# A hybrid decoder layer on one core: a new order of its opening, its small vectors fetched first on another queue, and the last product block's last columns summed in two banks

## The chip, the cores and the metric
One core of one Trainium2 chip runs one layer in one launch. The metric is the device time in microseconds (us). Of the core's engines, PE (TensorE) multiplies matrices and turns tiles, DVE (VectorE) does elementwise work and sums, ACT (ScalarE) does activations and copies, POOL (GpSimd) does little here, and SP issues nearly all DMAs. Each engine takes its instructions in the order in which they were written. All times below are us from the start of the profile's span, if nothing else is said.

## The reference
`x` is 256 tokens by 1024 features, `c` one vector of 1024. All is float32.

```python
mod = silu(c) @ w_ada + b_ada                       # (1024) @ (1024 x 9216), cut into nine vectors
sh1, sc1, gt1, sh2, sc2, gt2, sh3, sc3, gt3 = split(mod, 9)
y = rmsnorm(h, norm_ffn1) * (1 + sc1) + sh1
h = h + 0.5 * gt1 * swiglu(y, w_ffn1_gu, w_ffn1_down)        # 1024 -> 2816 -> 1024
y = rmsnorm(h, norm_mix) * (1 + sc2) + sh2
q, k, v, gu, gv = split(y @ w_in)                   # 5 x 512
attn = causal_attention(rope(q), rope(k), v)        # 8 heads of 64; one block of 256 covers all tokens
gmlp = gelu(gu) * (tril(w_s) @ layernorm(gelu(gv)) + b_s)    # chunks of 128 tokens
h = h + gt2 * (concat(rmsnorm(attn), rmsnorm(gmlp)) @ w_out)
y = rmsnorm(h, norm_ffn2) * (1 + sc3) + sh3
h = h + 0.5 * gt3 * swiglu(y, w_ffn2_gu, w_ffn2_down)
return rmsnorm(h, norm_final)
```

## The kernel before
The 256 tokens are two tiles `t` of 128. The 1024 features are eight slices `j` of 128. Every weight block of 128 x 1024 is fetched once (512 KB, by SP, into one of eight `raw` tiles) and split into two float32r parts: ACT copies it to `wh`, DVE subtracts to get `wl`. The operand is split likewise (`yh`, `yl`), and a product of 512 columns is three matmuls into one PSUM bank: `wh` with `yh`, `wh` with `yl`, `wl` with `yh` (`mm3`, L383). `wh` and `wl` have ten places each.

**Opening.** The modulation of the first norm (`sh1`, `sc1`) comes slice by slice: for each slice two `w_ada` blocks arrive, DVE multiplies each with `c_row` and sums along the row (`ada_sum`), and two tiny operations make the shift and scale columns (`ada_col`). Meanwhile x is squared and summed (`open_s`), the reciprocal root is taken on POOL (`rstd_of`, L349), x is scaled (`open_x`, tile `xn`), turned by PE into tiles `px` (`open_t`), copied to `xnT`, and modulated by ACT into `yh` and `y` (`open_y`), from which DVE makes `yl` (`open_l`). The first four of the eleven gate/up blocks are multiplied slice by slice (`open_m`): 4 blocks x 2 tiles x 8 slices x 3 = 192 matmuls named `f`, into eight banks. `open_e` and `open_d` fetch, `open_g` makes `wh`, `open_G` makes `wl`, `open_A` begins the activation, and `open_p` turns the identity into a scratch bank, which produces nothing. The order of all these steps is the text `OPEN`: one word per step, and each engine runs what falls to it in that order.

**After the opening** come the other seven gate/up blocks and the down products of the first FFN, then the mixing part, whose order is the text `MIX`, then the second FFN. There, helper `tick()` places the splits and the sums for later gates between the products. In the mixing part `step_gb` makes the gated tile `g` on DVE, `step_gq` takes its mean square on ACT (`mean_sq`) and its root by `rstd_of`, `step_gw` scales it, and `step_mt` has PE turn it (tile `tr_mg`).

**End.** The last three blocks' down products run token tile by token tile and half by half (L1028). After the 18 matmuls of a half, `Chain.residual` (L472) runs on it: DVE multiplies the bank by the gate and adds to `h`, ACT squares and sums, DVE multiplies by the final norm's row. After the second half come the root and the scaling, and the two halves are stored.

`rstd_of` adds eps on DVE where it is given two partial sums, and on POOL where it is given one:

```python
        if len(parts) == 2:
            vec.tensor_scalar(v, parts[0], parts[1], EPS, op0=ALU.add, op1=ALU.add)
        else:
            nc.gpsimd.tensor_scalar(v, parts[0], EPS, None, op0=ALU.add)
        nc.gpsimd.tensor_tensor(r, v, mhalf, op=ALU.pow)
```

In the profile's names L85 is the helper through which all DVE and PE work is written, so tiles are read there by name.

Of the kernel before, what the change touches and what calls it, by code (L numbers as in the profile page):

```python
# [38 lines left out]
d.1.0 p p p p x.0.0.1.a a.0.0 p p t.0.a p p c.0.0 p p p p p p p p p c.1.0 p g.0.0.0.2.v p y.0 p x.1.1.3.v G.0.0.0.1 p
p p k d.1.1 p l.0 G.0.0.1.1 p p g.0.1.0.1.a m.0.0.0.0 a.0.1 a.1.1 c.0.1 c.1.1 e.1.2 g.0.1.1.1.a m.0.0.1.1 G.0.1.0.2  # L40
t.2.a g.1.0.0.2.a e.0.2 y.1 p t.3.v d.2.0 t.1.a l.1 p m.0.1.1.1 p m.0.1.0.1 g.1.1.0.2.a d.2.1 m.0.1.1.0 G.1.0.0.1
m.0.1.0.0 G.1.0.1.1 g.2.0.0.1.a G.1.1.0.1 p m.1.0.0.1 g.2.0.1.1.a m.1.1.0.1 a.1.2 m.1.0.1.0 c.1.2 a.0.2 m.1.0.0.0
G.1.1.1.1 c.0.2 m.0.0.0.1 g.2.1.0.1.a G.2.0.0.1 e.1.3 G.2.0.1.1 m.1.1.1.0 y.2 d.3.0 l.2 g.2.1.1.1.a e.0.3 e.1.4 d.3.1
e.0.4 G.2.1.0.1 G.2.1.1.1 a.1.3 g.3.0.0.1.a g.3.0.1.1.a m.1.1.0.0 m.2.0.1.1 m.1.1.1.1 m.2.1.0.1 a.0.3 c.1.3 c.0.3
d.4.0 m.0.0.1.0 y.3 m.2.0.0.0 m.2.1.1.0 d.4.1 m.2.1.0.0 G.3.0.0.2 m.1.0.1.1 l.3 a.1.4 e.0.5 m.2.0.1.0 m.3.0.1.0
m.3.0.0.0 g.3.1.0.2.a G.3.1.1.1 G.3.1.0.1 e.1.5 m.3.1.1.1 d.5.0 m.2.1.1.1 d.5.1 m.3.1.1.0 c.1.4 a.0.4 g.4.0.0.2.a
c.0.4 e.1.6 y.4 m.3.0.1.1 g.4.1.1.1.a G.4.0.0.2 m.2.0.0.1 g.4.1.0.1.a l.4 m.3.1.0.1 G.4.1.0.2 a.1.5 m.3.1.0.0
m.3.0.0.1 e.0.6 m.4.1.1.1 g.5.0.0.2.a m.4.1.0.1 d.6.0 c.1.5 m.4.0.1.1 m.4.0.1.0 a.0.5 c.0.5 y.5 g.5.1.0.2.a m.4.1.1.0
m.4.0.0.1 d.6.1 m.4.0.0.0 G.5.0.0.2 l.5 m.5.0.0.1 e.1.7 m.5.0.1.0 m.5.0.1.1 G.5.1.1.1 g.6.0.0.2.a G.5.1.0.1 m.5.1.0.1
a.1.6 m.5.0.0.0 a.0.6 m.5.1.1.0 m.4.1.0.0 c.1.6 c.0.6 G.6.0.1.1 e.0.7 m.5.1.1.1 G.6.0.0.1 y.6 l.6 m.5.1.0.0 m.6.0.1.1  # L50
d.7.0 a.1.7 g.6.1.0.2.a G.6.1.0.2 a.0.7 m.6.0.1.0 d.7.1 c.1.7 g.7.0.1.1.a m.6.0.0.0 c.0.7 g.7.0.0.1.v m.6.0.0.1
m.6.1.0.0 G.7.0.0.1 y.7 g.7.1.0.2.a l.7 m.6.1.1.0 G.7.0.1.1 u m.6.1.0.1 m.6.1.1.1 G.7.1.0.1 G.7.1.1.1 m.7.0.0.1
# [1047 lines left out]
```

## Time and profile before

| what | us |
|---|---|
| median of three runs (511.62, 511.62, 513.96) | 511.62 |
| span of the profiled execution, first to last instruction | 509.2 |
| median less span: what lies around the span | 2.4 |
| PE busy in the span | 496.5 (98%) |
| DVE busy | 375.1 (74%) |
| ACT busy | 264.1 (52%) |
| POOL busy | 24.3 (5%) |

The profile gives one execution instruction by instruction. A row of its timeline begins with the start and the duration, then the engine, the line, the operation, what it writes and reads, the sizes, and in brackets how long the engine had been idle before it and who ended that. A row of the chain of waits has a start, a length and what filled it. A row of the view by stretches has, for each engine, busy time and in brackets the number of instructions.

### The profile page before, as it was taken

What the parts mean: (1) busy time and instruction counts of PE and PEld (TensorE: products, weight loads), DVE (VectorE), ACT (ScalarE), POOL (GpSimd) and SP (SyncE); (2) the same over time, 40 slices, a digit from 0 to 9 for tenths busy, and PEclk for the clock granted to TensorE, in tenths of its full rate; (3) what the DMA queues carried; (4) which work ended last, traced back from release to release, by engine and by line L of the source; (5) the groups of instructions that cost most, each with busy time, mean ns of one, the idle gap of its engine ahead of it and who ended that gap; (6) DMA issues with size and microseconds to landing.
All of it is one profiled execution on the core that took longest, in us unless ns stands there. A gap on an engine that the chain in (4) does not pass through costs nothing.

```text
span 509.2 us, 6450 instructions
## 1 busy us (share of the span) xinstructions
PE 496.5 (98%) x2297; PEld 404.7 (79%) x2297; DVE 375.1 (74%) x512; ACT 264.1 (52%) x405; POOL 24.3 (5%) x38
## 2 busy tenths in 40 slices
...
GB/s 281 398 371 376 328 236 340 413 408 325 338 308 314 362 208 207 136 196 322 259 258 242 240 196 287 215 325 331 340 205 189 187 168 202 181 152 1 0 2 82
DMA packets 38018, 126.38 MB, mean 248 GB/s; under 512 B 4449, under 2 KB 4449, under 8 KB 37986
## 3 DMA queue, kind: packets, MB, share of 16 engines
...
## 4 chain that ended last, share of the span: by engine, by line
PE 92%; DVE 2%; issue 2%; DMA 1%; ACT 1%; POOL 1%; SPq 0%; POOLq 0%; ACTq 0%
PE pg L85 39%; PE po L85 21%; PE f L85 8%; PE pw L85 4%; PE pp_gv L85 2%; PE pp_v L85 2%; PE pp_q L85 2%; PE pp_k L85 2%; PE pp_gu L85 2%; PE pa L85 2%; PE psc L85 2%; DMA h<-in_x_dram 1%; PE pv L85 1%; PE pada L85 1%; PE ppT L85 1%
## 5 line engine op out<-in xcount | busy, mean ns | idle before, releaser
L85 PE MATMUL pg<-wh_gu,yh 128*128 128x512 f32 x288 | 115.4, 401 | 0.0
L85 DVE TENSOR_TENSOR wl_gu<-raw_gu,wh_gu 128x1024 fp32r<-128x1024 f32 x72 | 86.8, 1222 | 38.1 <-ACT wh_gu L209 37.9
L85 PE MATMUL pg<-wl_gu,yh 128*128 128x512 f32 x288 | 113.7, 395 | 0.0
L85 PE MATMUL pg<-wh_gu,yl 128*128 128x512 f32 x288 | 113.6, 394 | 0.0
L209 ACT ACTIVATE wh_gu<-raw_gu 128x1024 fp32r<-128x1024 f32 x72 | 74.4, 1055 | 49.3 <-PE po L85 30.6
L85 DVE TENSOR_TENSOR wl_d<-raw_d,wh_d 128x1024 fp32r<-128x1024 f32 x44 | 53.8, 1227 | 28.2 <-ACT wh_d L209 28.1
L85 PE MATMUL po<-wh_d,ah 128*128 128x512 f32 x176 | 69.1, 393 | 0.0
L85 PE MATMUL po<-wh_d,al 128*128 128x512 f32 x176 | 69.0, 392 | 0.0
L85 PE MATMUL po<-wl_d,ah 128*128 128x512 f32 x176 | 69.0, 392 | 0.0
L209 ACT ACTIVATE wh_d<-raw_d 128x1024 fp32r<-128x1024 f32 x44 | 46.4, 1059 | 35.0 <-PE pg L85 25.1
L85 PEld LDWEIGHTS pg<-wl_gu,yh 128*128 128x128 f32 x288 | 54.2, 188 | 12.7
L85 PEld LDWEIGHTS pg<-wh_gu,yl 128*128 128x128 f32 x288 | 54.3, 189 | 11.8
L85 PEld LDWEIGHTS pg<-wh_gu,yh 128*128 128x128 f32 x288 | 54.3, 189 | 11.8
L85 PEld LDWEIGHTS po<-wh_d,ah 128*128 128x128 f32 x176 | 33.1, 188 | 7.2
L85 PEld LDWEIGHTS po<-wl_d,ah 128*128 128x128 f32 x176 | 33.1, 188 | 7.1
L85 PEld LDWEIGHTS po<-wh_d,al 128*128 128x128 f32 x176 | 33.1, 188 | 7.1
L85 DVE SCALAR_TENSOR_TENSOR ada<-ada,c_row 128x1024 f32<-128x1024 f32 x32 | 38.5, 1218 | 0.0
L85 DVE SCALAR_TENSOR_TENSOR acc<-ada,cols,acc 128x1024 f32<-128x1024 f32 x24 | 30.7, 1278 | 0.1
L422 ACT ACTIVATE sg<-pg 128x256 f32<-128x256 f32 x36 | 13.7, 385 | 31.6 <-PE pg L85 31.6
L434 ACT ACTIVATE ah<-pa 128x512 fp32r<-128x512 f32 x22 | 13.2, 598 | 26.1 <-PE pa L85 26.1
L85 PE MATMUL f<-wl_first,yh 128*128 128x512 f32 x64 | 25.4, 396 | 0.9 <-DVE wl_first L85 0.9
L85 PE MATMUL f<-wh_first,yh 128*128 128x512 f32 x64 | 25.6, 400 | 0.0
...
## 6 DMA issues: line engine op xcount, KB each, us to landing
raw_gu<-in_gu_dram SPq DMA_DIRECT2D x72, 512.0 KB, 4.8
raw_d<-in_w_ffn_down_dram SPq DMA_DIRECT2D x44, 512.0 KB, 5.2
ada<-in_w_shsc_dram SPq DMA_DIRECT2D x32, 512.0 KB, 5.0
ada<-in_w_gate_dram SPq DMA_DIRECT2D x24, 512.0 KB, 5.0
raw_ada<-in_w_shsc_dram SPq DMA_DIRECT2D x16, 512.0 KB, 6.8
raw_first<-in_gu_dram SPq DMA_DIRECT2D x16, 512.0 KB, 6.7
raw_wo<-in_w_out_dram SPq DMA_DIRECT2D x8, 512.0 KB, 4.4
raw_inq<-in_w_in_dram SPq DMA_DIRECT2D x4, 512.0 KB, 6.8
```

Source lines behind the costliest of these rows:

```text
L85: return getattr(self.engine, name)(out, *args, **kw)
L209: nc.scalar.activation(wh[:, :n], raw[:, :n], AF.Copy)
L422: nc.scalar.activation(sg, ps[:, 0:256], AF.Silu)
L434: nc.scalar.activation(ah, pv, AF.Copy)
```

## The change
1. `cols` (all small vectors) is fetched first, on ACT's queue and not as third on SP's; the two halves of x follow each other on SP.
2. `OPEN` is written anew. The products go strictly slice by slice, gate/up blocks in pairs. The squares of both token tiles are on DVE and all scaling of x is on ACT. All four turns of x stand together ahead of the first product, with 22 idle turns ahead of them and 5 behind; the idle turns between the products are gone.
3. The turn of x (`open_t`) and the copy out of PSUM (`open_q`) are steps of their own, and slice 0 is modulated straight from the PSUM tile (`open_y`).
4. In slice 0 the matmul with `yl` is the last of the three.
5. The three `1 + scale` operations become one, placed behind the squares; silu of the column form of c goes behind the second slice.
6. `rstd_of` adds eps on DVE in all cases.
7. At the end, in the last half of the last token tile, the last block's products go to two new banks of 256 columns each (12 matmuls of 256 in place of 6 of 512). The residual of the blocks before it is added to `h` on its own, then each 256 columns get their own residual, square and norm row, and three partial sums are added in two steps. The square writes over the residual's scratch tile.
8. Comments are dropped, which moves lines (L85 becomes L84).

```diff
 OPEN = """
-s.1.v p e.1.0 p p p p p p s.0.a p p p p p e.0.0 p p p d.0.0 e.1.1 p x.1.0.1.v e.0.1 p p p d.0.1 x.0.1.3.a a.1.0 p p
...
+e.1.0 e.0.0 d.0.0 d.0.1 s.0.v e.1.1 e.0.1 d.1.0 s.1.v e.1.2 x.0.0.1.a b x.0.1.3.a a.1.0 x.1.0.1.a a.0.0 e.0.2 p p p p
+p p p p p p p p p p p p p p p p p p t.0 x.1.1.3.a c.1.0 c.0.0 t.1 g.0.0.0.1.a d.1.1 t.2 G.0.0.0.1 y.0 t.3 p p p p p
+q.1.v l.0 m.0.0.0.0 g.0.0.1.1.a m.0.0.0.1 q.0.a G.0.0.1.1 q.3.a q.2.v g.0.1.0.1.a m.0.0.1.0 d.2.0 g.0.1.1.1.a
...
-    nc.sync.dma_start(c_one, i["c"])
-    nc.sync.dma_start(h[0], i["x"][0, tsl(0), :])
-    nc.sync.dma_start(cols, i["cols"])
-    nc.sync.dma_start(h[1], i["x"][0, tsl(1), :])
+    nc.scalar.dma_start(cols, i["cols"])
+    nc.sync.dma_start(c_one, i["c"])
+    for t in range(NT):
+        nc.sync.dma_start(h[t], i["x"][0, tsl(t), :])
...
-            nc.gpsimd.tensor_scalar(v, parts[0], EPS, None, op0=ALU.add)
+            vec.tensor_scalar(v, parts[0], EPS, None, op0=ALU.add)
...
-    def mm3(ps, lh, ll, wh, wl, first, last):
+    def mm3(ps, lh, ll, wh, wl, first, last, low_last=False):
+        rest = [(ll, wh), (lh, wl)]
+        if low_last:
+            rest.reverse()
         ten.matmul(ps, lh, wh, start=first, stop=False)
-        ten.matmul(ps, ll, wh, start=False, stop=False)
-        ten.matmul(ps, lh, wl, start=False, stop=last)
+        ten.matmul(ps, *rest[0], start=False, stop=False)
+        ten.matmul(ps, *rest[1], start=False, stop=last)
...
+    def open_q(j, e):
         xnT[j] = op.tile([P, 2, S], F32, tag="xT", name=f"xnT{j}")
+        ks = slice(1 if j == 0 else 0, 2)
         if e == "v":
-            vec.tensor_copy(xnT[j], pv)
+            vec.tensor_copy(xnT[j][:, ks, :], px[j][:, ks, :])
...
-            nc.scalar.activation(d, xnT[j // 2][:, j % 2, :], AF.Identity,
+            nc.scalar.activation(d, (xnT[j // 2] if j else px[0])[:, j % 2, :], AF.Identity,
                                  scale=adacol[1][:, js], bias=adacol[0][:, js])
...
     for t in range(NT):
+        c = Chain(t, "z")
+        z = [unit(f"zo{t}{n}", [P, 512]) for n in range(2)]
+        def add(n, po, o, square=True):
+            s = slice(n * 512 + o.start, n * 512 + o.stop)
+            tmp = unit(f"res_z{t}{s.start}", [P, o.stop - o.start])
+            vec.tensor_tensor(tmp, po, adarow[8][:, s], op=ALU.mult)
+            vec.tensor_tensor(h[t][:, s], h[t][:, s], tmp, op=ALU.add)
+            if square:
+                c.parts.append(mean_sq(h[t][:, s], D, f"z{t}{s.start}", tmp))
+                vec.tensor_tensor(z[n][:, o], h[t][:, s], nrow["nfin"][n][:, o], op=ALU.mult)
         for n in range(2):
-            for b in range(NB - HOLD, NB):
+            apart = (t, n) == (NT - 1, 1)
+            for b in range(NB - HOLD, NB - 1 if apart else NB):
...
+            add(n, f2.po[t][n], slice(0, 512), not apart)
+        if apart:
+            for q in range(2):
+                o = slice(q * 256, q * 256 + 256)
+                pe = psm(f"pe{q}")[:, 0:256]
+                for k in range(2):
+                    ah, al = f2.a[last]
+                    wh, wl = need(("d2", last, k))
+                    mm3(pe, ah[:, k, tsl(t)], al[:, k, tsl(t)], wh[:, 512 + o.start:512 + o.stop],
+                        wl[:, 512 + o.start:512 + o.stop], k == 0, k == 1)
+                add(1, pe, o)
+            v = sm.tile([P, 1], F32, tag="var", name=f"v2_z{t}")
+            vec.tensor_tensor(v, c.parts[0], c.parts[1], op=ALU.add)
+            c.parts = [v, c.parts[2]]
```

**DVE at the start, before** (`h_81` is the second half of x, `xn` its scaled copy, `raw_ada` a block of `w_ada`, `wh_first`/`wl_first` the split of a gate/up block):

```order
L85 SCALAR_TENSOR_TENSOR xn_115,ss_x_116<-h_81 128x1024
L85 TENSOR_SCALAR xn_115<-h_81,r_x_119 128x256
L85 SCALAR_TENSOR_TENSOR raw_ada_0_124,sum_163<-raw_ada_0_124,c_row 128x1024
L85 SCALAR_TENSOR_TENSOR raw_ada_0_144,sum_174<-raw_ada_0_144,c_row 128x1024
L85 TENSOR_TENSOR ada_col_187<-sum_174,cols 128x1
L85 SCALAR_TENSOR_TENSOR ada_col_198<-sum_163,cols 128x1
L85 CAST wh_first_0_201<-raw_first_0_149 128x1024
L85 TENSOR_SCALAR xn_115<-h_81,r_x_119 128x768
L85 TENSOR_TENSOR wl_first_0_202<-raw_first_0_149,wh_first_0_201 128x512
```

and in the changed kernel:

```order
L84 SCALAR_TENSOR_TENSOR xn_119,ss_x_120<-h_80 128x1024
L84 TENSOR_SCALAR v_x_122<-ss_x_120 128x1
L84 SCALAR_TENSOR_TENSOR xn_132,ss_x_133<-h_81 128x1024
L84 TENSOR_SCALAR v_x_135<-ss_x_133 128x1
L84 TENSOR_SCALAR cols<-cols 128x3x8
L84 SCALAR_TENSOR_TENSOR raw_ada_0_111,sum_144<-raw_ada_0_111,c_row 128x1024
L84 SCALAR_TENSOR_TENSOR raw_ada_0_113,sum_147<-raw_ada_0_113,c_row 128x1024
L84 SCALAR_TENSOR_TENSOR ada_col_180<-sum_144,cols 128x1
L84 TENSOR_TENSOR ada_col_182<-sum_147,cols 128x1
L84 TENSOR_TENSOR wl_first_0_190<-raw_first_0_115,wh_first_0_189 128x512
L84 COPY xnT_213<-px_184 128x512
L84 TENSOR_TENSOR yl<-y_0_200,yh 128x256
```

Both squares and the eps now stand on DVE; both scalings of x and the first `wh` copy have left it.

**DVE in the mixing part, before** (`g_2731` and `g_2757` are the gated tiles of the two token tiles, `o_2711` the attention output of the second, `pmx` the gate's products in PSUM):

```order
L85 TENSOR_TENSOR g_2731<-g_2731,ug_2660 128x512
L85 SCALAR_TENSOR_TENSOR o_2711<-o_2711,r_o_2723,row_g_attn_out 128x512
L85 TENSOR_TENSOR g_2757<-pmx_2702,cols 128x256
L85 TENSOR_TENSOR g_2757<-pmx_2726,cols 128x256
L85 TENSOR_TENSOR g_2757<-g_2757,ug_2696 128x512
L85 SCALAR_TENSOR_TENSOR g_2731<-g_2731,r_g_2747,row_g_gmlp_out 128x512
```

and in the changed kernel:

```order
L84 TENSOR_TENSOR g_2697<-g_2697,ug_2626 128x512
L84 TENSOR_SCALAR v_g_2712<-ss_g_2709 128x1
L84 SCALAR_TENSOR_TENSOR o_2677<-o_2677,r_o_2689,row_g_attn_out 128x512
L84 TENSOR_TENSOR g_2723<-pmx_2668,cols 128x256
L84 TENSOR_TENSOR g_2723<-pmx_2692,cols 128x256
L84 TENSOR_TENSOR g_2723<-g_2723,ug_2662 128x512
L84 TENSOR_SCALAR v_g_2730<-ss_g_2727 128x1
L84 SCALAR_TENSOR_TENSOR g_2697<-g_2697,r_g_2713,row_g_gmlp_out 128x512
```

The two `v_g`, which need the square that ACT takes of the `g` just made, have come from POOL into DVE's row.

**DVE at the end, before** (from the last bank of the last token tile on):

```order
L85 TENSOR_TENSOR res_z_4464<-po_3322,ada_row_3447 128x512
L85 TENSOR_TENSOR h_81<-h_81,res_z_4464 128x512
L85 TENSOR_TENSOR zo_4470<-h_81,nfin_3457 128x512
L85 TENSOR_SCALAR v_z_4472<-ss_z_4459,ss_z_4467 128x1
L85 TENSOR_SCALAR zo_4462<-zo_4462,r_z_4473 128x512
```

and in the changed kernel (`pe` are the two new banks):

```order
L84 TENSOR_TENSOR res_z_4422<-po_3288,ada_row_3413 128x512
L84 TENSOR_TENSOR h_81<-h_81,res_z_4422 128x512
L84 TENSOR_TENSOR res_z_4432<-pe_4425,ada_row_3413 128x256
L84 TENSOR_TENSOR h_81<-h_81,res_z_4432 128x256
L84 TENSOR_TENSOR zo_4385<-h_81,nfin_3423 128x256
L84 TENSOR_TENSOR res_z_4445<-pe_4438,ada_row_3413 128x256
L84 TENSOR_TENSOR h_81<-h_81,res_z_4445 128x256
L84 TENSOR_TENSOR zo_4385<-h_81,nfin_3423 128x256
L84 TENSOR_TENSOR v_z_4451<-ss_z_4407,ss_z_4435 128x1
L84 TENSOR_SCALAR v_z_4453<-v_z_4451,ss_z_4448 128x1
```

Five operations behind the bank have become ten, six of them half as wide.

## Rows read from the trace of the kernel before

**Rows 1.** View by stretches: PE, PEld, DVE, ACT, POOL, PEclk, DMA share, GB/s.

```profile
30.00:40.00 10.00, 10.00 (x45) 8.11 (x44) 9.31 (x19) 5.66 (x9) 0.00 (x0) 1.00 1.03 388
200.00:480.00 280.00, 279.71 (x1325) 229.08 (x1325) 201.97 (x259) 156.78 (x253) 13.81 (x18) 1.00 0.63 213
```

**Rows 2.** Chain of waits in order of time, opening.

```profile
16.40 2.29 DVE raw_ada L85 x4
18.86 1.23 DVE wl_first L85
...
22.95 40.44 PE f L85 x174
63.39 4.18 PE pg L85 x18
```

**Rows 3.** Timeline of DVE: the square of the second half of x.

```profile
7.34 1.22 DVE L85 SCALAR_TENSOR_TENSOR xn<-h 128x1024 f32<-128x1024 f32 x1 [1.91 <-DMA h<-in_x_dram]
```

**Rows 4.** Timeline of POOL: the two roots of x.

```profile
8.98 0.57 POOL L357 TENSOR_TENSOR r_x<-v_x,mhalf 128x1 f32<-128x1 f32 x1
10.10 1.40 POOL L357 TENSOR_TENSOR r_x<-v_x,mhalf 128x1 f32<-128x1 f32 x1
```

**Rows 5.** Timeline of ACT: x scaled, modulated, and first split copies.

```profile
11.53 1.33 ACT L592 ACTIVATE xn<-h,r_x 128x768 f32<-128x768 f32 x2 [3.58 <-POOL r_x L357]
...
14.24 0.60 ACT L631 ACTIVATE yh<-xnT,ada_col,ada_col 128x256 fp32r<-128x256 f32 x1
...
15.29 1.16 ACT L654 ACTIVATE wh_first<-raw_first 128x512 fp32r<-128x512 f32 x2
```

**Rows 6.** Timeline of PE: the first product.

```profile
15.51 0.48 PE L85 MATMUL f<-wh_first,yh 128*128 128x512 f32 x1
```

**Rows 7.** Groups of the stretch 13 to 60 by form: count, busy, mean ns, idle before.

```profile
L85 DVE SCALAR_TENSOR_TENSOR raw_ada<-raw_ada,c_row 128x1024 f32<-128x1024 f32 x14 | 16.8, 1218 | 0.0
L85 DVE TENSOR_TENSOR wl_first<-raw_first,wh_first 128x512 fp32r<-128x512 f32 x20 | 13.0, 686 | 0.6 <-ACT wh_first L654 0.5
...
L85 DVE TENSOR_TENSOR yl<-y,yh 128x256 fp32r<-128x256 f32 x8 | 3.4, 424 | 0.2 <-ACT y L631 0.2
```

**Rows 8.** DMA issues of 3.4 to 3.6: count, KB, us from issue to landing.

```profile
raw_first<-in_gu_dram SPq DMA_DIRECT2D x1, 512.0 KB, 7.8
```

**Rows 9.** View by stretches of the idle turns alone (PE, PEld, PEclk, DMA, GB/s).

```profile
8.00:9.00 1.00, 1.00 (x7) 1.00 (x6) 1.00 0.99 404
...
10.00:11.00 1.00, 1.00 (x9) 1.00 (x9) 1.00 1.04 379
```

**Rows 10.** Timelines of DVE, ACT and PE round the gated tiles.

```profile
288.90 0.75 DVE L85 SCALAR_TENSOR_TENSOR o<-o,r_o,row_g_attn_out 128x512 f32<-128x512 f32 x1
...
290.35 0.69 DVE L85 TENSOR_TENSOR g<-g,ug 128x512 f32<-128x512 f32 x1
290.96 0.74 DVE L85 SCALAR_TENSOR_TENSOR g<-g,r_g,row_g_gmlp_out 128x512 f32<-128x512 f32 x1
...
289.02 0.63 ACT L365 ACTIVATE j_g<-g 128x512 f32<-128x512 f32 x1 [1.80 <-DVE g L85]
...
291.99 0.60 PE L85 MATMUL tr_mg<-ident,g 128*128 128x128 f32 x4
```

**Rows 11.** Timelines of PE, DVE and ACT at the end, and two 256-column operations.

```profile
501.27 0.40 PE L85 MATMUL po<-wh_d,al 128*128 128x512 f32 x1
501.71 0.69 DVE L85 TENSOR_TENSOR res_z<-po,ada_row 128x512 f32<-128x512 f32 x1 [1.98 <-PE po L85]
...
503.16 0.63 ACT L365 ACTIVATE j_z<-h 128x512 f32<-128x512 f32 x1 [3.40 <-DVE h L85]
...
503.92 0.21 DVE L85 TENSOR_SCALAR v_z<-ss_z,ss_z 128x1 f32<-128x1 f32 x1
...
484.77 0.39 ACT L422 ACTIVATE sg<-pg 128x256 f32<-128x256 f32 x1 [1.02 <-PE pg L85]
485.19 0.42 DVE L85 TENSOR_TENSOR a<-sg,pg 128x256 f32<-128x256 f32 x1 [0.98 <-ACT sg L422]
```

More of the change, by code (lines that the diff above doesn't have):

```diff
@@ L37 @@
 OPEN = """
-s.1.v p e.1.0 p p p p p p s.0.a p p p p p e.0.0 p p p d.0.0 e.1.1 p x.1.0.1.v e.0.1 p p p d.0.1 x.0.1.3.a a.1.0 p p
[L39 to L52, printed above, removed]
@@ L53 @@
-A.0.0.1 m.7.0.0.0 A.0.0.0 w.1 m.7.1.0.1 m.7.0.1.0 m.7.0.1.1 m.7.1.0.0 m.7.1.1.0 m.7.1.1.1 A.1.0.0 w.0 A.1.1.0 A.0.1.0
-w.3 w.2 A.0.1.1 A.1.0.1 A.1.1.1
+e.1.0 e.0.0 d.0.0 d.0.1 s.0.v e.1.1 e.0.1 d.1.0 s.1.v e.1.2 x.0.0.1.a b x.0.1.3.a a.1.0 x.1.0.1.a a.0.0 e.0.2 p p p p
+p p p p p p p p p p p p p p p p p p t.0 x.1.1.3.a c.1.0 c.0.0 t.1 g.0.0.0.1.a d.1.1 t.2 G.0.0.0.1 y.0 t.3 p p p p p
+q.1.v l.0 m.0.0.0.0 g.0.0.1.1.a m.0.0.0.1 q.0.a G.0.0.1.1 q.3.a q.2.v g.0.1.0.1.a m.0.0.1.0 d.2.0 g.0.1.1.1.a
+G.0.1.0.1 m.0.0.1.1 G.0.1.1.1 m.0.1.0.0 a.1.1 e.1.3 m.0.1.0.1 g.1.0.0.1.a m.0.1.1.0 g.1.0.1.1.a a.0.1 e.0.3 m.0.1.1.1
@@ new lines @@
+c.1.1 c.0.1 d.2.1 G.1.0.0.1 y.1 z k l.1 G.1.0.1.1 m.1.0.0.0 g.1.1.0.1.a a.1.2 m.1.0.0.1 d.3.0 g.1.1.1.1.a m.1.0.1.0
+G.1.1.0.1 g.2.0.0.2.a e.1.4 m.1.0.1.1 G.1.1.1.1 a.0.2 m.1.1.0.0 e.0.4 m.1.1.0.1 c.1.2 c.0.2 m.1.1.1.0 d.3.1 G.2.0.0.2
+y.2 m.1.1.1.1 l.2 d.4.0 a.1.3 g.2.1.0.2.a m.2.0.0.0 m.2.0.0.1 G.2.1.0.2 e.1.5 g.3.0.0.2.a m.2.0.1.0 m.2.0.1.1 a.0.3
+e.0.5 m.2.1.0.0 c.1.3 m.2.1.0.1 c.0.3 d.4.1 G.3.0.0.2 y.3 m.2.1.1.0 m.2.1.1.1 l.3 d.5.0 a.1.4 g.3.1.0.2.a m.3.0.0.0
+m.3.0.0.1 G.3.1.0.2 e.1.6 m.3.0.1.0 g.4.0.0.2.a m.3.0.1.1 a.0.4 e.0.6 m.3.1.0.0 c.1.4 m.3.1.0.1 c.0.4 d.5.1 G.4.0.0.2
@@ new lines @@
+y.4 m.3.1.1.0 m.3.1.1.1 l.4 d.6.0 a.1.5 m.4.0.0.0 g.4.1.0.2.a m.4.0.0.1 G.4.1.0.2 e.1.7 m.4.0.1.0 g.5.0.0.2.a
+m.4.0.1.1 a.0.5 e.0.7 m.4.1.0.0 c.1.5 m.4.1.0.1 c.0.5 d.6.1 G.5.0.0.2 y.5 m.4.1.1.0 m.4.1.1.1 l.5 d.7.0 a.1.6
+m.5.0.0.0 g.5.1.0.2.a m.5.0.0.1 G.5.1.0.2 d.7.1 m.5.0.1.0 g.6.0.0.2.a m.5.0.1.1 a.0.6 m.5.1.0.0 c.1.6 m.5.1.0.1 c.0.6
+G.6.0.0.2 y.6 m.5.1.1.0 m.5.1.1.1 l.6 a.1.7 m.6.0.0.0 g.6.1.0.2.a m.6.0.0.1 G.6.1.0.2 m.6.0.1.0 g.7.0.0.2.a m.6.0.1.1
+a.0.7 m.6.1.0.0 g.7.1.0.2.a c.1.7 m.6.1.0.1 c.0.7 G.7.0.0.2 y.7 m.6.1.1.0 m.6.1.1.1 l.7 u G.7.1.0.2 m.7.0.0.0
@@ L55 @@
+m.7.0.0.1 w.0 w.1 m.7.0.1.0 m.7.0.1.1 A.0.0.0 A.0.0.1 A.0.1.0 A.0.1.1 w.2 m.7.1.0.0 m.7.1.0.1 A.1.0.0 A.1.0.1
+m.7.1.1.0 m.7.1.1.1 A.1.1.0 A.1.1.1 w.3
 """
@@ L173, in tile_decoder_layer @@
         nc.scalar.activation(c_row[:, nsl(n)], p, AF.Silu)
-    nc.scalar.activation(c_col, c_col, AF.Silu)
-    for comp in (1, 4, 7):
-        vec.tensor_scalar(b_sc[comp], b_sc[comp], 1.0, None, op0=ALU.add)
     ident = const.tile([P, P], F32, name="ident")
```

27 lines of the change are left out of this document (13 added, 14 removed).

## The prediction, made before the changed kernel was run
> **What bounds the kernel now.** I read the view by stretches first. From 200 to 480 us PE is busy 279.71 of 280 us, and from 30 to 40 us all the time, with DVE close behind (9.31 of 10) and the DMA engines full (share 1.03 at 388 GB/s) [rows 1]. The reader is to see that PE sets the time and that only the first 20 us have other limits. The chain of waits says where the change-over is: behind the DVE sums and split, 174 opening products run without a gap from 22.95 for 40.44 us, and at 63.39 the next block's products follow at once [rows 2]. One product takes 40.44/174 = 0.2324 us. All 192 take 44.6 us, so the opening ends as if they had started at 63.39 - 44.6 = 18.8 with no hole. Then PE has no hole worth naming until the last product, and behind that stands a chain of DVE, ACT and POOL to the store [rows 11]. So the change can move the time in three ways alone: the end of the opening, a new hole in PE's stream, and the chain at the end. All other work it moves lies beside PE.
>
> **The opening.** I walk the new order with durations from the rows.
>
> *x and the first slice.* The second half of x was there at 7.32 (DVE had waited for it) [rows 3]. It now stands third on SP, not fourth, so one issue earlier at best; I keep 7.34. The square takes 1.22, the eps about 0.2 (as v_z [rows 11]), `1 + scale` 0.1: DVE is free for the first sum at 8.9. In the queue's third place a block landed at 3.5 + 7.8 = 11.3 [rows 8], and 512 KB at 388 GB/s take 1.35 [rows 1], so the first two blocks are there at 8.6 and 9.95. A sum takes 2.29/2 = 1.15, the two columns 0.2 [rows 2]: columns ready at 11.5. The second tile's root runs on POOL from 8.9 beside a sum. One root took 0.57 while DVE waited for it, the other 1.40 while DVE was in a sum [rows 4]; I take 1.40, so 10.3. ACT scales in 1.33 [rows 5], to 11.6 (before: 12.86), makes the first `wh` half (0.6) and `yh` (0.6) and PE can start at 12.8, where before it started at 15.51 [rows 6]. `y` ends at 13.25, and DVE, which has split (0.65) and copied in between, has `yl` at 13.95 [rows 7]. That `yl` now goes last in slice 0 is worth one product there, and modulating from PSUM takes a copy of 0.6 off the way to the first product; both lie in these figures.
>
> *DVE up to slice 2.* A 512-column split costs 13.0/20 = 0.65, `yl` 0.42 [rows 7]. From 13.95: split, copy, two splits (2.6) 16.55; two sums and columns (2.5) 19.05; split; `yl` of slice 1 must wait for ACT's `yh` and `y` (1.1 behind the columns), 20.6; split, sum, two splits, sum, columns (0.65 + 1.15 + 1.3 + 1.15 + 0.25) 25.1; a 1024-wide split 1.2 and `yl` 0.35, 26.65. PE's slices of 24 products last 5.58 each: slice 0 is done at 19.1 and slice 1, held by `yl` at 20.6, at 26.0, so slice 2 is held once more, by `yl` at 26.65. From there DVE needs per slice two sums (2.3), two splits (2.4), `yl` and columns (0.6), 5.3 in all, less than PE's 5.58: PE leads no more. The DMA engines need 4 x 1.35 = 5.4. PE then has 143 products left: 26.7 + 143 x 0.2324 = 59.9, and I take 60.0. Gain against 63.39: **3.4**. Bounds: 4 if x lands earlier and the root takes 0.57; 1 if the hand-overs between DVE and ACT cost 0.3 more in each of the eight slices. I stay near the walk, since its rows are those of the same instructions on the same engines.
>
> *Cover.* The other seven DVE and ACT steps that move lie beside these. The small vectors' issue on ACT is hidden by ACT's wait for c's products; without that cover it would cost one DMA issue. The mask, the later fetches and the first activations keep their order against PE.
>
> **The mixing part.** With the eps on DVE, six more tiny operations (0.1 each) stand in DVE's row. For four of them the input is there when DVE arrives. The two `v_g` are different: they wait for ACT's square of the `g` that DVE has only just made. Before, DVE went straight on with o (288.90), the second g (290.35) and the scaled g (290.96), and PE turned that at 291.99, 0.3 after it was done at 291.70 [rows 10]. From the start of a square to an eps on DVE takes 503.92 - 503.16 = 0.76 [rows 11]. So: square at 289.1, `v_g` at 289.87, o at 289.95, the second g's last step 1.45 later as before at 291.4, its square 0.72 later at 292.1, the second `v_g` at 292.9, the scaled g from 292.95 to 293.7, PE's turn at 293.8. Queued behind are that scaled g and all of DVE; PE waits **1.8**. Bounds: 0, if PE's row let it do something else (it does not), and 2.1 with the 0.3 of cover gone. DVE makes the delay up afterwards, as its sums for later gates have room.
>
> **The end.** The twelfth product of the last half starts six steps ahead of the last (501.27), at 499.9. DVE starts 0.44 behind a product [rows 11], at 500.35. Two dependent 512-wide operations take 503.16 - 501.71 = 1.45 [rows 11]: the sum into `h` starts at 501.07, the first 256 columns' product with the gate 0.65 behind it, at 501.7. A dependent 256-wide operation takes 0.42 + 0.03 [rows 11]: `h` 502.15, norm row 502.6, then (not dependent, 0.37) the second 256 columns at 503.0, `h` 503.4, square 503.85. The square of 256 columns is about 0.2 shorter than that of 512 (0.39 against 0.6 for an ACT operation, [rows 5, 11]): eps at 503.85 + 0.56 = 504.4, before 503.92. The end comes **0.5 later**: the narrower last piece saves 0.75 behind the last product, but DVE is still at work on the pieces ahead of it, so DVE and not PE is what the last piece waits for. Bounds: -0.75 if DVE were free, +0.9 if a 256-wide operation cost as much as a wide one beside these.
>
> **Sum:** -3.4 + 1.8 + 0.5 = -1.1. The sum stands on the span 509.2; the median is 2.4 above it, which the change does not touch: 511.6 - 1.1 = **510.5**.
>
> **The rivals.**
> *The v_g wait costs PE nothing.* For it: PE has other products near, and its turn has 0.3 to spare. Against: PE's row is in order, and the scaled g stands behind both waits. Time: 511.6 - 3.4 + 0.5 = 508.7.
>
> *Transfers pace the slices.* PE's 5.58 per slice, the DMA engines' 5.4 and DVE's 5.3 lie close. A block is fetched only when DVE has freed a place, in one order, so a late sum delays a later block. If each of slices 2 to 7 comes 0.35 late, the opening gains 1.3 and the time is 512.6. Against it: PE never waited there before at the same bandwidth.
>
> *Slower: TensorE stays at 1.2 GHz.* The idle turns ran 7 per us between 8 and 9 and 9 per us between 10 and 11 [rows 9]: there PE went up to 2.4 GHz, with nothing but turns behind it since before 8. Now 22 turns stand there, not 27, and a gap of about 1 us before x's turns. It decides if the higher level is not there by about 18, as stalls hide what comes before. If it came at 26, a product would take about 0.46 until then: 26 products from 13.95 to 26, then 165 at 0.2324, end 64.3, 4.3 later: 514.8. The Trainium skill ("TensorE: Matmul & The Clock Gate", Part 4: PE-mode transpose) says that transposes don't count as work for the clock as matmuls do, which would put the rise behind the products' start. By that rule the case is this rival; the trace disagrees, for the rise came amid idle turns. The products of slice 0 fill PE in any case, so I hold this unlikely.
>
> **How the numbers follow.** A measurement of this kernel can tell about 0.5%, 2.6 us, from no change: faster means under 509.1, slower over 514.2. The forecast (all three terms as above) gets 0.64, the hidden `v_g` 0.18, the transfers 0.13, the clock 0.05. The forecast's own spread of about 1.3 either way puts 0.04 of it under 509.1 and 0.02 of the others' weight over 514.2. So faster 0.22, same 0.71, slower 0.07. The range takes in the first two rivals: 508.4 to 512.7, leaving out about 0.1 at either side.
>
> **What would show it.** Right: first product near 12.8, `yl` of slice 2 near 26.6, the first product of the fifth block near 60 (not 63.39); one PE hole of 1.5 to 2 before the turn of the gated tile, with DVE idle twice for ACT's square; eps of the last tile 3.1 behind the last wide product's start and DVE busy without a break from that product on. Wrong: PE waiting for `wl_first` again in slices 3 to 7, no hole at the gated tile, idle or product spacing of 0.4 in the opening, or the last piece waiting for PE.

## The result and the profile after

The changed kernel takes **509.55 us** (median of 5 runs, 509.33 to 509.75), the kernel before 511.62 beside it (5 runs, 511.35 to 513.96). The ratio is 0.9947, its 95% interval 0.9927 to 0.9966: faster by 0.5%. The forecast was 510.5, 1.0 too high, with 508.4 to 512.7 as its range; by its own line for "faster", under 509.1, this is "same", which it had given 0.71. The span of the profiled execution went from 509.2 to 507.6.

The opening first. The chain of waits of the changed kernel (start, length, what filled it):

```profile
25.71 33.59 PE f L84 x143
59.29 4.19 PE pg L84 x18
```

The fifth block starts at 59.29, not at 63.39 [rows 2]: **4.1 earlier**, where 3.4 was forecast. The last gap in PE's row is where it was expected, ahead of the 143 products that need `yl` of slice 2. The timeline of DVE shows where the further 0.7 is from:

```profile
4.53 1.22 DVE L84 SCALAR_TENSOR_TENSOR xn<-h 128x1024 f32<-128x1024 f32 x1 [2.76 <-DMA h<-in_x_dram]
...
5.87 1.22 DVE L84 SCALAR_TENSOR_TENSOR xn<-h 128x1024 f32<-128x1024 f32 x1
...
8.00 1.23 DVE L84 SCALAR_TENSOR_TENSOR raw_ada<-raw_ada,c_row 128x1024 f32<-128x1024 f32 x1 [0.63 <-DMA raw_ada<-in_w_shsc_dram]
...
25.23 0.43 DVE L84 TENSOR_TENSOR yl<-y,yh 128x256 fp32r<-128x256 f32 x1
```

The row at 5.87 has no bracket: when DVE had squared the first half of x, the second was there. Before, DVE waited for it until 7.34 [rows 3]. The first sum starts at 8.00 (forecast 8.9) and waits 0.63 for its block, no longer for x; the block itself had been put at 8.6. `yl` of slice 2 is done at 25.66 (25.23 + 0.43; forecast 26.65, held by rows that had been put 0.9 later from the start). Slower products (0.235, 33.59/143, not 0.232) take 0.36 of this 1.0 back, and the forecast had rounded up to 60.0. PE's first product comes at 13.05 (forecast 12.8, before 15.51 [rows 6]), and it does not matter that it is late, since slices 1 and 2 wait for `yl` all the same.

The mixing part, timeline of the changed kernel (DVE, ACT and PE in order of time):

```profile
285.72 0.15 DVE L84 TENSOR_SCALAR v_g<-ss_g 128x1 f32<-128x1 f32 x1 [0.79 <-ACT j_g L361]
285.79 0.74 DVE L84 SCALAR_TENSOR_TENSOR o<-o,r_o,row_g_attn_out 128x512 f32<-128x512 f32 x1
...
287.96 0.63 ACT L361 ACTIVATE j_g<-g 128x512 f32<-128x512 f32 x1 [2.27 <-DVE g L84]
...
288.71 0.15 DVE L84 TENSOR_SCALAR v_g<-ss_g 128x1 f32<-128x1 f32 x1 [0.79 <-ACT j_g L361]
288.78 0.74 DVE L84 SCALAR_TENSOR_TENSOR g<-g,r_g,row_g_gmlp_out 128x512 f32<-128x512 f32 x1
...
289.67 0.63 PE L84 MATMUL tr_mg<-ident,g 128*128 128x128 f32 x4 [1.63 <-DVE g L84]
```

DVE stands idle for ACT's square twice, 0.79 each time, and PE's turn of the gated tile, which before followed without a wait [rows 10], waits 1.63. The turn has moved from 291.99 to 289.67, only 2.32 earlier, where the opening had given 4.10: **1.78 lost**, 1.8 forecast.

The end. The twelfth product of the last half, in PE's timeline of the kernel before:

```profile
499.90 0.39 PE L85 MATMUL po<-wh_d,al 128*128 128x512 f32 x1
```

and the timeline of PE, DVE and ACT in the changed kernel, from its twelfth product on:

```profile
497.78 0.39 PE L84 MATMUL po<-wh_d,al 128*128 128x512 f32 x1
...
499.31 0.28 PE L84 MATMUL pe<-wl_d,ah 128*128 128x256 f32 x1
499.55 0.42 DVE L84 TENSOR_TENSOR res_z<-pe,ada_row 128x256 f32<-128x256 f32 x1
...
500.80 0.42 DVE L84 TENSOR_TENSOR res_z<-pe,ada_row 128x256 f32<-128x256 f32 x1
...
501.71 0.42 ACT L361 ACTIVATE res_z<-h 128x256 f32<-128x256 f32 x1 [0.74 <-DVE h L84]
...
502.31 0.21 DVE L84 TENSOR_SCALAR v_z<-v_z,ss_z 128x1 f32<-128x1 f32 x1
```

PE's last product starts at 499.31, but DVE takes up the last 256 columns only at 500.80, after an unbroken row of its own work: up to the eps, four operations of DVE behind the last wide bank have become ten. The twelfth product has moved from 499.90 to 497.78, 2.12 earlier; the eps at 502.31 is 1.61 earlier than at 503.92 [rows 11]. So the end lost **0.51** (forecast 0.5). In the span: -4.10 + 1.78 + 0.51, and 0.2 of differences between the turn and the twelfth product that were not traced, make -1.6.

### The profile page after: what moved, and what is told of

Read it like the earlier page. It is cut to its first block, busy times and chain, and to the rows that moved or that the text cites. A ratio compares the mean times of both kernels' runs of the same rounds, so it can differ in the third digit from the quotient of the medians.

```text
span 507.6 us, 6405 instructions
## 1 busy us (share of the span) xinstructions
PE 494.5 (97%) x2279; PEld 402.5 (79%) x2279; DVE 376.5 (74%) x517; ACT 266.4 (52%) x406; POOL 21.5 (4%) x30
## 4 chain that ended last, share of the span: by engine, by line
PE 92%; DVE 3%; issue 2%; ACT 1%; DMA 0%; POOL 0%; POOLq 0%; ACTq 0%
PE pg L84 40%; PE po L84 21%; PE f L84 8%; PE pw L84 4%; PE pp_gv L84 2%; PE pp_v L84 2%; PE pp_k L84 2%; PE pp_gu L84 2%; PE pp_q L84 2%; PE pa L84 2%; PE psc L84 2%; PE pv L84 1%; PE idle L84 1%; PE pc L84 1%; DVE g L84 1%
## 5 line engine op out<-in xcount | busy, mean ns | idle before, releaser
L84 PE MATMUL pg<-wh_gu,yh 128*128 128x512 f32 x288 | 115.4, 401 | 0.0
L84 DVE TENSOR_TENSOR wl_gu<-raw_gu,wh_gu 128x1024 fp32r<-128x1024 f32 x72 | 86.9, 1223 | 37.4 <-ACT wh_gu L205 37.2
L84 PE MATMUL pg<-wl_gu,yh 128*128 128x512 f32 x288 | 113.7, 395 | 0.0
L84 PE MATMUL pg<-wh_gu,yl 128*128 128x512 f32 x288 | 113.6, 394 | 0.0
L84 DVE TENSOR_TENSOR wl_d<-raw_d,wh_d 128x1024 fp32r<-128x1024 f32 x44 | 53.6, 1224 | 30.0 <-ACT wh_d L205 29.9
L84 PE MATMUL po<-wh_d,ah 128*128 128x512 f32 x174 | 68.5, 394 | 0.0
L84 PE MATMUL po<-wl_d,ah 128*128 128x512 f32 x174 | 68.2, 392 | 0.0
L84 PE MATMUL po<-wh_d,al 128*128 128x512 f32 x174 | 68.2, 392 | 0.0
L84 PEld LDWEIGHTS pg<-wl_gu,yh 128*128 128x128 f32 x288 | 54.2, 188 | 12.7
L84 PEld LDWEIGHTS pg<-wh_gu,yl 128*128 128x128 f32 x288 | 54.3, 189 | 11.9
L84 PEld LDWEIGHTS pg<-wh_gu,yh 128*128 128x128 f32 x288 | 54.3, 189 | 11.8
L84 DVE SCALAR_TENSOR_TENSOR ada<-ada,c_row 128x1024 f32<-128x1024 f32 x32 | 38.5, 1218 | 0.0
L84 PEld LDWEIGHTS po<-wh_d,al 128*128 128x128 f32 x174 | 32.7, 188 | 7.2
L84 PEld LDWEIGHTS po<-wh_d,ah 128*128 128x128 f32 x174 | 32.7, 188 | 7.1
L84 PEld LDWEIGHTS po<-wl_d,ah 128*128 128x128 f32 x174 | 32.7, 188 | 7.0
L84 DVE SCALAR_TENSOR_TENSOR acc<-ada,cols,acc 128x1024 f32<-128x1024 f32 x24 | 30.7, 1278 | 0.1
L84 PE MATMUL f<-wh_first,yl 128*128 128x512 f32 x64 | 25.6, 399 | 0.5 <-DVE yl L84 0.5
L84 PE MATMUL f<-wh_first,yh 128*128 128x512 f32 x64 | 25.4, 397 | 0.0
```

The source lines that it names most:

```text
L84: return getattr(self.engine, name)(out, *args, **kw)
```

## The experiments

The theory after the result: three terms that add, -4.1 or more from the opening, +1.8 from `v_g` on DVE, +0.5 from the split end, and the opening's excess over the forecast comes from x's second half landing earlier. The rivals stand in each expectation. Medians in us, range and number of runs; the kernel before took 511.62 to 511.83 (medians) beside them:

| run | what differs | median | runs |
|---|---|---|---|
| after | | 509.55 | 509.33 to 509.75, 5 |
| e1 | changed kernel, eps of later norms on POOL | 507.65 | 507.41 to 507.72, 6 |
| e2 | changed kernel, old end | 509.12 | 508.87 to 509.52, 6 |
| e3 | both: new opening alone | 507.21 | 506.70 to 507.87, 5 |
| e4 | changed kernel, small vectors between x's halves | 510.71 | 509.53 to 511.70, 12 |
| b1 | kernel before, later eps on DVE | 513.51 | 511.84 to 514.46, 12 |
| b2 | kernel before, small vectors first | 509.60 | 509.44 to 510.08, 8 |
| n1 | changed kernel, no idle turns | 509.57 | 509.19 to 510.08, 8 |
| z1 | changed kernel, last norm product late | 509.51 | 509.11 to 509.86, 7 |
| z2 | changed kernel, last norm product with the root | 509.05 | 508.88 to 509.57, 5 |
| f1 | e3, copies moved | 507.11 | 507.07 to 507.35, 4 |
| f2 | f1, `yl` last in slices 1 and 2 | 507.16 | 507.09 to 507.56, 4 |

**e1: the eps back on POOL.** In `rstd_of`:

```diff
-            vec.tensor_scalar(v, parts[0], EPS, None, op0=ALU.add)
+            e = vec if name[0] == "x" else nc.gpsimd
+            e.tensor_scalar(v, parts[0], EPS, None, op0=ALU.add)
```

> The changed kernel with one edit: the single-part eps goes back to POOL for every norm but x's. Theory (the wait of v_g on DVE for ACT's square holds the scaled g, and PE with it): PE's wait at the turn of the gated tile goes, 1.8 us less, so 509.55 - 1.8 = 507.8, and DVE has no idle time behind j_g. Rival (the hole is made by DVE being full there whatever the eps does, or PE's hole is filled later): 0 to 0.3 less, about 509.4.

Measured 507.65, 1.9 less. The timeline of e1 has DVE go straight through, with the eps on POOL beside it, and the turn has no bracket:

```profile
285.14 0.75 DVE L84 SCALAR_TENSOR_TENSOR o<-o,r_o,row_g_attn_out 128x512 f32<-128x512 f32 x1
...
286.07 0.22 POOL L353 TENSOR_SCALAR v_g<-ss_g 128x1 f32<-128x1 f32 x1 [1.50 <-ACT j_g L362]
...
287.20 0.74 DVE L84 SCALAR_TENSOR_TENSOR g<-g,r_g,row_g_gmlp_out 128x512 f32<-128x512 f32 x1
...
288.23 0.60 PE L84 MATMUL tr_mg<-ident,g 128*128 128x128 f32 x4
```

The scaled g is 1.58 earlier than in the changed kernel (288.78), although e1's opening had ended 0.3 later in its profiled execution (fifth block at 59.62). The turn is 1.44 earlier, with that 0.33 1.77. The theory holds.

**b1: the same edit from the other side**, the kernel before with the eps of every norm but x's on DVE:

> The kernel before with one part of the change alone: the single-part eps of every norm but x's on DVE. Theory (v_g holds DVE's row for ACT's square): a new wait of PE of 1.6 at the turn of the gated tile, where before there was none, and 1.8 more: 511.8 + 1.8 = 513.6. Rival (the 1.8 seen so far belongs to the shifted schedule of the changed kernel, not to the eps): 0, 511.8.

Measured 513.51, 1.9 over the median beside it; the ratio is 1.0026, which is 1.3 more, with the interval 1.0010 to 1.0041, 0.5 to 2.1 more. The timeline of PE in b1 has a wait at the turn that the kernel before does not have, and the chain has the start of the fifth block:

```profile
295.14 0.63 PE L85 MATMUL tr_mg<-ident,g 128*128 128x128 f32 x4 [1.64 <-DVE g L85]
```

```profile
64.75 4.19 PE pg L85 x18
```

The turn is 3.15 later than in the kernel before (291.99 [rows 10]). The opening, which the edit does not touch, had ended 1.36 later in this execution (64.75 against 63.39 [rows 2]; the reason stands under e4 and b2), so 1.79 of it arose behind the opening. The wait belongs to the eps and not to the shifted schedule.

**e2 and e3: the old end, alone and with e1's edit.** The last loop of the kernel before takes the place of the new one:

```diff
-        if apart:
-            for q in range(2):
...
-                add(1, pe, o)
...
+        for n in range(2):
+            c.residual(n, f2.po, adarow[8])
```

> The changed kernel with the last half summed in one bank again, as before the change. Theory (the split costs 0.5, as DVE and not PE is what the last piece waits for): 0.5 less, 509.05, and the eps of the last tile comes 4.0 behind the start of the 12th product of the last half, not 4.5. Rival (the split saves the 0.75 of the narrower last piece): 0.7 more, 510.3.

> The changed kernel with both edits: eps of the later norms on POOL and the old end, so that the new opening alone is left. Theory (three terms that add): 1.8 + 0.5 = 2.3 less, 507.25, which is 4.4 under the kernel before: 4.1 in the span and the rest around it. Rival (terms not independent: PE's hole in the mixing part let DVE catch up, so taking it away makes a new wait): 508 to 509.

Measured 509.12 and 507.21, both near the theory: the split end costs 0.4 by the medians, and the terms add, since the old end is worth 0.4 with the eps on POOL too (507.65 to 507.21) and the eps 1.9 with the old end too (509.12 to 507.21). The runs of e2 and of the changed kernel overlap a little; the timeline of e2, twelfth product and eps of the last tile, is clearer:

```profile
498.00 0.39 PE L84 MATMUL po<-wh_d,al 128*128 128x512 f32 x1
...
502.01 0.21 DVE L84 TENSOR_SCALAR v_z<-ss_z,ss_z 128x1 f32<-128x1 f32 x1
```

The eps comes 4.01 behind the twelfth product, as expected, where the changed kernel has 4.53 (497.78 to 502.31). e3 beats both kernels, by 4.4 and 2.3.

**e4 and b2: the fetch of the small vectors**, put back between x's halves in the changed kernel, and put first in the kernel before (with the other steps as they were):

```diff
-    nc.scalar.dma_start(cols, i["cols"])
     nc.sync.dma_start(c_one, i["c"])
-    for t in range(NT):
-        nc.sync.dma_start(h[t], i["x"][0, tsl(t), :])
+    nc.sync.dma_start(h[0], i["x"][0, tsl(0), :])
+    nc.sync.dma_start(cols, i["cols"])
+    nc.sync.dma_start(h[1], i["x"][0, tsl(1), :])
```

> The changed kernel with one edit: the small vectors are fetched on SP's queue between the two halves of x again. Theory (their place ahead of x's second half is what made that half land at 5.9 and not at 7.3; my forecast had kept 7.34 and its walk gave 60.0 for the first product of the fifth block): DVE waits for x until about 7.3 again, the fifth block starts 0.7 later (60.0), total 510.2. Rival (the second half lands early for another reason, or the chain behind it has slack): 0 to 0.2 more. Time around the span: if the shorter time outside the span (1.7 against 2.4) comes from the queue of this fetch, it goes back to 2.4, another 0.6.

> The kernel before with one part of the change alone: the small vectors fetched first, on ACT's queue, and the two halves of x next to each other on SP. Theory (x's second half then lands near 5.9, and the roots, the scaled x and the sums behind it move up with it): DVE's square 1.4 earlier than at 7.34, the first product near 14.1 instead of 15.5, 1.4 less in the span; with the 0.8 by which the median of the kernel before lies above its profiled execution (511.8 - 1.7 - 509.2) 2.2 less in all, 509.6, and a spread of the runs under 1 us in place of 3. Rival (the old order of steps has its own limits, ACT's square of the first half at 6.81 and the sums' blocks, so that an earlier half is not used): 0 to 0.5 less, 511.5.

Measured 510.71 (1.2 more than the changed kernel, 0.7 expected) and 509.60 (2.0 less than the kernel before, 2.2 expected). The square of x's second half in DVE's timeline, and the chain behind it, in e4:

```profile
8.11 1.22 DVE L84 SCALAR_TENSOR_TENSOR xn<-h 128x1024 f32<-128x1024 f32 x1 [2.17 <-DMA h<-in_x_dram]
```

```profile
27.18 33.50 PE f L84 x143
60.68 4.19 PE pg L84 x18
```

and in b2:

```profile
6.08 1.22 DVE L85 SCALAR_TENSOR_TENSOR xn<-h 128x1024 f32<-128x1024 f32 x1 [2.70 <-DMA h<-in_x_dram]
```

```profile
21.68 40.43 PE f L85 x174
62.11 4.19 PE pg L85 x18
```

With the 44 KB of small vectors ahead of it on its queue, the second half came at 7.34 to 8.11; without, by 5.87 and 6.08. In b2 the fifth block moved by 1.28 (63.39 to 62.11) for an x that came 1.26 earlier (7.34 to 6.08): the old order of steps used all of it. And e4 bears out the rest of the forecast's walk, which had put the fifth block at 60.0 for an x at 7.34: x came 0.77 later than that, the block 0.68. Against the changed kernel x is 2.24 later and the block only 1.39, since in the changed kernel the first sum waits for its own block.

The runs also differ in spread. The three kernels with the fetch between x's halves range over 4.0 (before, 22 runs beside b1), 2.2 (e4) and 2.6 us (b1), all others over 0.3 to 1.2. b1's trace shows one reason, TensorE's clock. Below stand DVE's square of x's second half and PE's 20 idle turns between x's first turns and the first product, and then the granted clock from 14 to 16 (view by stretches: PE, granted clock, DMA share, GB/s):

```profile
7.49 1.23 DVE L85 SCALAR_TENSOR_TENSOR xn<-h 128x1024 f32<-128x1024 f32 x1 [2.10 <-DMA h<-in_x_dram]
...
13.66 3.92 PE L85 MATMUL idle<-ident 128*128 128x128 f32 x20
```

```profile
14.00:16.00 2.00, 2.00 (x11) 0.50 1.07 404
```

and the same in the kernel before:

```profile
13.41 2.35 PE L85 MATMUL idle<-ident 128*128 128x128 f32 x20
```

```profile
14.00:16.00 2.00, 2.00 (x19) 1.00 1.06 401
```

In b1 x came only 0.15 later, but PE, which had waited 1.92 for the scaled x (1.60 in the kernel before), had hardly gone on with x's turns at 13.07 when the granted clock fell, at about 13.5, to 0.50, which is 1.2 GHz. The 20 idle turns took 3.92 in place of 2.35, the first product came at 17.33 in place of 15.51, and the opening ended 1.36 later. In b2 x's turns follow the idle turns at once, without that wait, and so they do in the changed kernel. The mean granted clock on record for each of the 22 runs of the kernel before beside b1 points the same way: the ten over 512.5 have 0.989 to 0.994, the twelve under 511.7 have 0.995 to 0.998. So the fetch takes away not only 1.3 of x's delay but also a wait behind which the clock can fall. That it fell in just those ten runs is not shown, since only single executions were seen instruction by instruction; nor is how much of the spread comes from x's landing. What besides the wait decides it stays open too: n1 below waits longer ahead of x's turns (2.36 and 0.75), and its granted clock reads 1.00.

**n1: no idle turns.** In `OPEN`:

```diff
-... e.0.2 p p p p p p p p p p p p p p p p p p p p p p t.0 ...
+... e.0.2 t.0 ...
...
-... t.3 p p p p p q.1.v ...
+... t.3 q.1.v ...
```

> The changed kernel without its 27 idle turns. If the idle turns are what takes TensorE to 2.4 GHz by the first product: the first products follow each other at 0.46 instead of 0.232 us for some us, slice 0 ends 1 to 2 us later than 18.7, but since slices 1 and 2 wait for DVE's yl (19.8 and 25.7) only 0 to 0.6 of it reaches the end: 509.6 to 510.2. If the clock is up without them (c's products alone): product spacing 0.232 from the first, x's turns up to 0.8 earlier, and 0 to 0.3 less, 509.3. The clock rival of my forecast in its strong form (level not there until 26 us): 4 more, 513.8.

Measured 509.57: nothing lost or gained that can be told. The timeline of PE in n1:

```profile
8.69 0.47 PE L82 MATMUL px<-ident,xn 128*128 128x128 f32 x1 [2.36 <-ACT xn L589]
9.92 3.19 PE L82 MATMUL px<-ident,xn 128*128 128x128 f32 x15 [0.75 <-ACT xn L589]
12.86 0.48 PE L82 MATMUL f<-wh_first,yh 128*128 128x512 f32 x1
13.18 0.39 PE L82 MATMUL f<-wl_first,yh 128*128 128x512 f32 x1
13.41 0.48 PE L82 MATMUL f<-wh_first,yl 128*128 128x512 f32 x1
13.73 0.40 PE L82 MATMUL f<-wh_first,yh 128*128 128x512 f32 x1
```

x's 15 turns take 3.19 here, 0.21 each, and 1.91 for 16 behind the idle turns of the changed kernel, 0.12 each. So x's turns are quicker behind the idle turns, but they then start later by as much: the first product comes at 12.86 and 13.05. The products follow each other by 0.23 to 0.32 from the first, near the 0.235 of the whole opening (33.59/143, at a granted clock of 1.00), not by 0.46.

**z1 and z2: what the end waits for.** Both leave the last half's `zo` out of `add`. z1 multiplies behind the eps:

```diff
         c.rstd()
+        if apart:
+            vec.tensor_tensor(z[1], h[t][:, nsl(1)], nrow["nfin"][1], op=ALU.mult)
```

z2 folds it into the scaling of the last tile:

```diff
-        vec.tensor_scalar(z[0], z[0], c.r, None, op0=ALU.mult)
-        nc.scalar.activation(z[1], z[1], AF.Copy, scale=c.r)
+        vec.scalar_tensor_tensor(z[1], h[t][:, nsl(1)], c.r, nrow["nfin"][1], op0=ALU.mult, op1=ALU.mult)
+        nc.scalar.activation(z[0], z[0], AF.Copy, scale=c.r)
```

> The changed kernel with the norm's product of the last half (zo) taken out from between the pieces and put behind the eps. Theory (DVE's row is what the last piece waits for; its matmuls are done near 499.6): the second piece's product with the gate starts 0.34 earlier, and 0.3 less in all: 509.25. Rival (the last piece waits for PE): 0.

> The changed kernel with the last half's norm product folded into the scaling: DVE multiplies the last half by the root and the norm row in one operation behind the root, ACT scales the first half. In z1 the eps came 0.5 earlier, but POOL's root took 0.93 instead of 0.55 while DVE's 512-wide product ran beside it, and the gain was lost. Theory (a two-input DVE operation beside it is what stretches POOL's root): here DVE stands still during the root, it takes 0.55 again, and 0.5 comes off: 509.05. Rival (the root's 0.93 is chance, or the end is bound elsewhere): root 0.9, 509.5.

z1 gained nothing that can be told (509.51). In its timeline DVE took up the second piece 2.56 behind the twelfth product, where the changed kernel took 3.02 (497.78 to 500.80). The eps came 4.01 behind it and not 4.53, but the root was longer:

```profile
498.09 0.39 PE L84 MATMUL po<-wh_d,al 128*128 128x512 f32 x1
...
500.65 0.42 DVE L84 TENSOR_TENSOR res_z<-pe,ada_row 128x256 f32<-128x256 f32 x1
...
502.10 0.21 DVE L84 TENSOR_SCALAR v_z<-v_z,ss_z 128x1 f32<-128x1 f32 x1 [0.51 <-ACT res_z L361]
502.23 0.68 DVE L84 TENSOR_TENSOR zo<-h,nfin 128x512 f32<-128x512 f32 x1
502.40 0.93 POOL L353 TENSOR_TENSOR r_z<-v_z,mhalf 128x1 f32<-128x1 f32 x1 [7.70 <-DVE v_z L84]
```

In z2 DVE does nothing while the root runs, and it takes 0.55 again:

```profile
498.29 0.39 PE L84 MATMUL po<-wh_d,al 128*128 128x512 f32 x1
...
502.30 0.21 DVE L84 TENSOR_SCALAR v_z<-v_z,ss_z 128x1 f32<-128x1 f32 x1 [0.51 <-ACT res_z L361]
502.59 0.55 POOL L353 TENSOR_TENSOR r_z<-v_z,mhalf 128x1 f32<-128x1 f32 x1 [7.69 <-DVE v_z L84]
503.18 0.75 DVE L84 SCALAR_TENSOR_TENSOR zo<-h,r_z,nfin 128x512 f32<-128x512 f32 x1 [0.66 <-POOL r_z L353]
```

The median is 509.05, as expected, but its five runs (508.88 to 509.57) overlap those of the changed kernel, so the time alone does not show the 0.5. The trace does: the eps comes 4.01 behind the twelfth product and the root ends 4.85 behind it, where the changed kernel has 4.53 and 5.38. The last piece waits for DVE, not for PE: with one operation of DVE less ahead of it, it starts 0.46 earlier behind the same products. With this the split end does as well as the old one (e2's root also ends 4.85 behind the twelfth product), not better.

**f1 and f2: is more to be had in the opening?** Both start from e3. In `OPEN` for both, and in `open_m` for f2 alone:

```diff
-... m.0.0.0.1 q.0.a G.0.0.1.1 q.3.a q.2.v g.0.1.0.1.a m.0.0.1.0 d.2.0 g.0.1.1.1.a
+... m.0.0.0.1 G.0.0.1.1 g.0.1.0.1.a m.0.0.1.0 d.2.0 g.0.1.1.1.a q.0.a q.3.a q.2.a
...
-        mm3(first[b, t], yh[:, j, tsl(t)], yl[:, j, tsl(t)], wh[:, c, :], wl[:, c, :], n == 1, n == KT, j == 0)
+        mm3(first[b, t], yh[:, j, tsl(t)], yl[:, j, tsl(t)], wh[:, c, :], wl[:, c, :], n == 1, n == KT, j < 3)
```

> The kernel of e3 (the new opening alone, median 507.2) with the copies of x's turned slices moved: all three that follow slice 0's first products go to ACT, behind its conversions for slice 0's second pair of blocks, so that DVE has one copy (0.68) less. Theory (what ends the opening now is DVE's row up to yl of slice 2, 8.0 to 25.2 almost without a wait): DVE's sums for slice 1 start 0.5 earlier and 0.3 to 0.5 comes off: 506.8. Rival (transfers pace it: in the trace of e3 ACT waited up to 1.9 for raw_first in slices 3 to 5 and the fifth block started at 60.3): 0, 507.2.

> The kernel of f1, and in slices 1 and 2 too the product with yl goes last of its three, as in slice 0. Theory (DVE's yl of slice 2 is the last hole): one product's worth, 0.2 less than f1, 506.6. Rival (transfers): 0 against f1.

507.11 and 507.16: no gain that can be told from e3 (507.21), so the theory's 0.3 to 0.5 is not borne out, and the traces speak for the rival. In f1 ACT waits longer for the weight blocks than in the changed kernel (0.79 at the same place), and passes some of it on to DVE:

```profile
20.72 1.16 ACT L664 ACTIVATE wh_first<-raw_first 128x512 fp32r<-128x512 f32 x2 [1.61 <-DMA raw_first<-in_gu_dram]
...
21.39 1.30 DVE L84 TENSOR_TENSOR wl_first<-raw_first,wh_first 128x512 fp32r<-128x512 f32 x2 [0.17 <-ACT wh_first L664]
...
25.20 0.43 DVE L84 TENSOR_TENSOR yl<-y,yh 128x256 fp32r<-128x256 f32 x1
```

`yl` of slice 2 comes at 25.20, where the changed kernel had it at 25.23. In f2 PE's hole ahead of it shrank to 0.2, but the transfers made one later, and the fifth block started at 59.69:

```profile
23.72 8.24 DMA raw_first<-in_gu_dram
37.36 22.34 PE f L84 x95
59.69 4.19 PE pg L84 x18
```

e3's profiled execution, with the same opening as the changed kernel, looks like f2's: its chain goes through a block's transfer from 23.92 to 32.56, and its fifth block started at 60.31. So with the fifth block at 59.3 to 60.3 the opening has come to where transfers pace it in some executions. The forecast's rival of that name did not decide this change, but it is what is late next.

## Why the forecast was right, and what was off

- **The mixing part**: +1.8 forecast, 1.78 in the trace, 1.9 by the medians of e1 and of b1 (1.3 by b1's ratio, 1.79 in its trace). The mechanism is the one forecast: an in-order row, a tiny operation that waits for another engine, and the wide operation that PE needs behind it. The rival that hid the wait (0.18) is out.
- **The end**: +0.5 forecast, 0.51 in the trace, 0.4 by e2. DVE and not PE is what the last piece waits for, as z1 and z2 show. One sign was worked out wrongly: the eps was to come 3.1 behind the last wide product's start, but the forecast's own times give 504.4 - 499.9 = 4.5, and 4.53 was measured.
- **The opening**: the mechanism held, but the sum's term was mis-sized, -3.4 against -4.1. The step that failed is "I keep 7.34" for x's second half. It was costed as one issue earlier at best; in fact the fetch ahead of it on the queue had held it, and it came by 5.87. The bound of 4 "if x lands earlier and the root takes 0.57" was nearly the case: one of the two roots ran beside DVE's square (the first, 1.46), the other with DVE idle.
- **Around the span**: "the median is 2.4 above it, which the change does not touch" was the second error. In the changed kernel and all eleven experiments the time of the profiled execution is 1.7 to 1.8 above its span, and so it is in each of the 48 runs of the kernel before beside the experiments. So the kernel before was profiled in an execution of about 510.9, 0.7 quicker than its median of 511.6. The 2.4 held this 0.7, which lies inside the spread that the change took away. No single trace of the kernel before could show it; b1's trace shows a part of where such a spread comes from.
- **The account**: -4.1 + 1.8 + 0.5 + 0.2 = -1.6 between the two profiled executions; less the 0.7 by which the kernel before was profiled under its median, and with the 0.2 by which the changed kernel was (509.33), -2.1, as measured. By medians the opening is worth 4.4 (e3; 4.6 against the runs beside it), of which the fetch alone gives 2.0 (b2) and the new order of steps another 2.4. The forecast was 1.0 too high: 0.7 by the opening and 0.5 by the two executions' place under their medians, less the 0.2 that was not traced.
- **The clock**: the slower rival is out for the changed kernel. Even without a single idle turn (n1) the products started at 0.23 to 0.32. But the forecast's reading of [rows 9] was weaker than it sounded: the granted clock is 1.00 in both of these stretches, and the rise was read from the count of turns alone. In the same way the changed kernel shows 1.00 throughout while its turns go from 0.21 each (4.69 for the 22 idle ones) to 0.12 (x's 16). b1's trace shows it in the clock itself: granted 0.50 from 14 to 16 and 1.00 from 17.0 to 17.3, with nothing but turns on PE from 13.07 to the first product at 17.33. The rule of the Trainium skill ("TensorE: Matmul & The Clock Gate", Part 4: PE-mode transpose), that transposes don't count as work for the clock as matmuls do, does not agree with that.
